# Gate tiles of an expert stage in two buffers, each loaded one four of experts ahead

## Chip, core and metric

The kernel runs on one core of a Trainium2 chip. The metric is the device time of one execution in microseconds; of several executions the median is taken. PE is the matrix engine (PEld its weight loads), DVE the vector engine, ACT the scalar engine, POOL the engine that issues the gathers, and SP the engine whose in-order queue issues all other DMAs.

## The reference, cut to what matters

One decoder layer over 1024 tokens and 16 meta tokens, width 1024: a mixer (latent attention and retention, merged by gates), then an expert layer with 16384 single-neuron experts. The expert layer is what matters here:

```python
x = rmsnorm(h, g_ffn)
# 8 heads choose 16 experts each by product keys: 128 indices eidx and 128 gates per token
act = gelu(einsum('td,tkd->tk', x, peer_u[eidx]))
y = einsum('tk,tkd->td', gates * act, peer_v[eidx])
out = h + y
```

## The kernel before, in words

The tokens are eight blocks of 128. Blocks 0 to 2 take the expert layer by **gathers**: for each of a block's 256 rows of `peer_u` and `peer_v`, POOL issues an indirect DMA of one row per token (tile `row`, four buffers, L1065) and DVE uses it (L1082, L1087). The gathers are background work: `pace` (called by `split_piece`, L221) puts a few of them behind every piece of weights that the main line splits.

Blocks 3 to 7 (640 tokens) take it **densely**, in `dense` (L1128). For each of 128 steps `e`, `scores(e)` (L1150) multiplies 128 experts' rows of `peer_u` with the 640 tokens on PE (line L246 to L248 with output tile `tr`) and writes gelu of it to a tile `gl` (three buffers, L1159). For the first 48 steps this is done early and stored in DRAM as `gl_d`, while `gate_matrix` (L1094) builds the gates of all experts for all 640 tokens in DRAM (`gate_d`). After that the **V stage** begins (`vp` pool, about 2057 us on). It takes 16 groups of eight steps in the order `es`, which mixes fours of steps whose `gl` is loaded from `gl_d` (12 fours) with fours whose scores are computed in this stage (20 fours). Per step:

- `activations(e)` (L1198) computes the scores or loads `gl`.
- `weights(e, gl)` (L1205): at the first step of a four it loads `gt`, the gates of four steps (1280 KB, 10 KB of each partition, DMA line L1209), then DVE multiplies `gl` by them (L1210). ACT rounds the product to `c_hi` and DVE takes the remainder `c_lo` (`split`, L218 and L219; eight buffers each).

When the eight steps of a group are prepared, PE multiplies `c_hi` and `c_lo` with pieces of `peer_v` (raw, three buffers; split to `whi` and `wlo`, three buffers) for the two halves of the width, in accumulators `zacc`, and DVE adds these to `y` (L1243). Each engine works through its own instructions in a fixed order, which the build takes from the program's order and a planner; SP's queue is in order too.

The gate tile has one buffer (`GTB = 1`, L46):

```python
            if e % 4 == 0:
                gt[0] = vp.tile([P, nt, 4, TS], F32, name="gt", bufs=GTB)
                nc.sync.dma_start(gt[0], gate_d[:, :, TS * e:TS * e + 4 * TS].rearrange("n p (e t) -> p n e t", e=4))
            V.tensor_tensor(gl.rearrange("p (n t) -> p n t", t=TS), gt[0][:, :, e % 4],
                            gl.rearrange("p (n t) -> p n t", t=TS), OP.mult)
```

Pools are stacks: `const`, `work`, `wp`, then on the left those of the mixer, and after them `up` (tiles `gl`), the pool of the gate matrix and `vp`. `work` stays open to the end; it holds `zt` (two buffers of 2 KB a partition; L251, L840), used by the mixer alone, and the four retention states (two buffers of 512 B each, L641), used by the mixer alone.

Of the kernel before, what the change touches and what calls it, by code (L numbers as in the profile page):

```python
# [12 lines left out]
F32 = mybir.dt.float32  # L13
BF16 = mybir.dt.bfloat16
# [9 lines left out]
P = 128  # L24
# [9 lines left out]
TW = 512  # L34
# [4 lines left out]
TS = 32  # L39
# [3 lines left out]
RING = 3  # L43
ROWS = 4
SPLIT = 3
GTB = 1  # L46
DELAY = 8.0
STEPS = (((86, 72), (116, 64), (116, 144)), ((112, 90), (112, 90), (112,)), (80, 50))
HEAD = 20
# [94 lines left out]
def hybrid_layer(ctx: ExitStack, tc: tile.TileContext, out, a, dbg=None):  # L144
    nc = tc.nc
    V, S, T, G = nc.vector, nc.scalar, nc.tensor, nc.gpsimd
# [3 lines left out]
    work = ctx.enter_context(tc.tile_pool(name="work", bufs=2))  # L150
    wp = ctx.enter_context(tc.tile_pool(name="wp", bufs=2))
    ps = ctx.enter_context(tc.tile_pool(name="ps", bufs=2, space=PSUM))
    dram = ctx.enter_context(tc.tile_pool(name="dram", bufs=1, space=DRAM))

    gat = ctx.enter_context(tc.tile_pool(name="gat", bufs=1, side="right"))


# [43 lines left out]
    gate_d = dram.tile([DT // TS, P, P * TS], F32, name="gate_d")  # L201
# [46 lines left out]
        T.matmul(o, st[1], mv[0], start=False, stop=last)  # L248

    def square_sum(src, acc):  # L250
        junk = work.tile([P, TW], F32, name="zt").bitcast(BF16)  # L251
        S.activation(junk[:, :src.shape[-1]], src, AF.Square, accum_out=acc)

    def norm_scale(tiles, name):
# [24 lines left out]
    def zacc(name="zacc"):  # L279
        return ps.tile([P, 2, 512], F32, name=name, tag="zacc", bufs=3)  # L280

    def tr():
        return ps.tile([P, TW], F32, name="tr", bufs=2)
# [20 lines left out]
    state = {}  # L304
# [11 lines left out]
    def group(g):  # L316
        blocks = GROUPS[g]
        nbk = len(blocks)
        W = P * nbk
# [270 lines left out]
        def retention(hp):  # L590
# [45 lines left out]
            def add_state(i):  # L636
                pst = tr()
                for s in range(2):
                    T.matmul(pst[64 * s:64 * s + 64, 0:P], qn[:, i, 128 + 64 * s:128 + 64 * s + 64],
                             vr[:, i, P * s:P * s + P], start=True, stop=True)  # L640
                new = work.tile([P, P], F32, name=f"state{hp}")  # L641
                if hp in state:
                    V.tensor_tensor(new, pst[:, 0:P], state[hp], OP.add)
                else:
                    V.tensor_copy(new, pst[:, 0:P])
                state[hp] = new
# [28 lines left out]
            th = rp.tile([P, nbk, 256], F32, name="at")  # L675
# [150 lines left out]
        def merge():  # L826
            mg = own.mg
            for c in range(KD):
                for s, src in enumerate((own.oTs, own.yTs)):
                    pz = zacc()  # L830
                    for j, w in enumerate(split_pieces(a["w_z"][2 * c + s], KD, P)):
                        mm3(pz[:, 0, :W], w, [t[:, j, :W] for t in own.hn], j == 0, j == KD - 1)
                        if j % 2:
                            yield
                    n = len(src)
                    for j, w in enumerate(split_pieces(a["w_ret" if s else "w_mla"][c], n, P)):
                        mm3(pz[:, 1, :W], w, src[j], j == 0, j == n - 1)
                        if j % 2:
                            yield
                    th = work.tile([P, TW], F32, name="zt")[:, :W]  # L840
                    S.activation(th, pz[:, 0, :W], AF.Tanh, scale=0.5)
                    V.scalar_tensor_tensor(th if s else mg[:, c], th, 1.0, pz[:, 1, :W], op0=OP.add, op1=OP.mult)
                    if s:
                        V.tensor_tensor(mg[:, c], mg[:, c], th, OP.add)
# [283 lines left out]
    def dense(xT):  # L1128
        nt = DT // TS
# [4 lines left out]
        for g, blocks in enumerate(GROUPS[NGROUP:-1]):  # L1134
            w = P * len(blocks)
            t = [xdp.tile([P, KD, w], F32R, name=f"x_{n}{g}") for n in ("hi", "lo")]
            per = 1024 // w
            for dst, src in zip(t, xT_d[g]):
                for j in range(0, KD, per):
                    n = min(per, KD - j)  # L1140
# [50 lines left out]
        vp = vps.enter_context(tc.tile_pool(name="vp", bufs=1, reuse_waits="tile"))  # L1191
        ys = []
        for b in range(NGATH, NBLK):
            ys.append(vp.tile([P, D], F32, name=f"y{b}"))
            nc.sync.dma_start(ys[-1], h2_d[b])
        gt = {}

        def activations(e):  # L1198
            if e >= AHEAD:
# [5 lines left out]
        def weights(e, gl):  # L1205

            if e % 4 == 0:
                gt[0] = vp.tile([P, nt, 4, TS], F32, name="gt", bufs=GTB)
                nc.sync.dma_start(gt[0], gate_d[:, :, TS * e:TS * e + 4 * TS].rearrange("n p (e t) -> p n e t", e=4))  # L1209
            V.tensor_tensor(gl.rearrange("p (n t) -> p n t", t=TS), gt[0][:, :, e % 4],  # L1210
                            gl.rearrange("p (n t) -> p n t", t=TS), OP.mult)
            hi = vp.tile([P, DT], F32R, name="c_hi", bufs=CB)
            lo = vp.tile([P, DT], F32R, name="c_lo", bufs=CB)
            split(hi, lo, gl)
            return hi, lo


        es = [4 * n + k for n in sorted(range(P // 4), key=lambda n: (n + 0.5) / AHEAD if 4 * n < AHEAD else
                                        (n + 0.5 - AHEAD / 4) / (P - AHEAD)) for k in range(4)]
        for e0 in range(0, P, GE):  # L1220
            group = es[e0:e0 + GE]
            ne = len(group)
# [65 lines left out]
    for n, now in enumerate(groups):  # L1288
        if n:
            now.open_mix()  # L1290
        now.mix()
        following = groups[n + 1] if n + 1 < len(groups) else None
        now.open_merge(following)
        interleave([now.merge()] + ([following.latents()] if following else []), STEPS[1][n])
        rest = now.output()
    dense(rest)
    finish(1)

# [17 lines left out]
```

## Time and profile before

| | us |
|---|---|
| median of 3 runs | 3613.85 (3611.62 to 3617.17) |
| profiled execution, its own time | 3618.72 |
| its span, first to last instruction | 3616.9 |
| PE busy | 3343.7 (92%) |
| DVE busy | 2788.3 (77%) |
| ACT busy | 1191.6 (33%) |
| POOL busy | 1088.5 (30%) |
| mean granted PE clock, share of full speed | 0.969 |

The span and the rows are those of the profiled execution; its time is 1.8 us longer than its span and 4.9 us longer than the median. Busy time of PE counts overlapping, pipelined instructions once.

### The profile page before, as it was taken

What the parts mean: (1) busy time and instruction counts of PE and PEld (TensorE: products, weight loads), DVE (VectorE), ACT (ScalarE), POOL (GpSimd) and SP (SyncE); (2) the same over time, 40 slices, a digit from 0 to 9 for tenths busy, and PEclk for the clock granted to TensorE, in tenths of its full rate; (3) what the DMA queues carried; (4) which work ended last, traced back from release to release, by engine and by line L of the source; (5) the groups of instructions that cost most, each with busy time, mean ns of one, the idle gap of its engine ahead of it and who ended that gap; (6) DMA issues with size and microseconds to landing.
All of it is one profiled execution on the core that took longest, in us unless ns stands there. A gap on an engine that the chain in (4) does not pass through costs nothing.

```text
span 3616.9 us, 54537 instructions
## 1 busy us (share of the span) xinstructions
PE 3343.7 (92%) x20376; PEld 3023.5 (84%) x20376; DVE 2788.3 (77%) x6698; ACT 1191.6 (33%) x2017; POOL 1088.5 (30%) x772
## 2 busy tenths in 40 slices
PE   8999989998799998999898899999999989999999
PEld 7888988788677898998888687888788878887788
DVE  5645569997896666899999887787778777877776
ACT  3445334544355533233333222222222222222221
POOL 0000000112011121113333355454545544544454
PEclk9999999999899998999999999999999999999999
DMA  3322454467644376455666788898889888988886
GB/s 128 119 81 98 136 189 136 150 211 242 209 145 154 123 261 242 160 174 218 267 252 259 273 313 315 286 321 293 303 281 315 279 288 297 323 298 287 287 298 247
DMA packets 329257, 837.18 MB, mean 231 GB/s; under 512 B 45712, under 2 KB 140688, under 8 KB 326176
## 3 DMA queue, kind: packets, MB, share of 16 engines
q1 hardware_dynamic: 218400, 431.00, 35.4%
q0 software_dynamic: 110592, 402.70, 31.5%
q8 instruction: 160, 2.62, 0.3%
q14 instruction: 105, 0.86, 0.1%
HBM read 755.16 MB, written 78.43 MB: 230 GB/s over the span
## 4 chain that ended last, share of the span: by engine, by line
PE 42%; DVE 20%; issue 16%; DMA 11%; POOL 8%; ACT 3%; POOLq 0%; SPq 0%; DVEq 0%; ACTq 0%
PE zacc L246 9%; PE zacc L248 9%; PE zacc L247 9%; POOL row L1065 8%; DMA row<-in_peer_v_dram,eidx 7%; DVE ob L1120 4%; DVE oa L1119 3%; DVE wlo L219 3%; DVE acc L1087 3%; PE tr L246 3%; PE tr L247 2%; PE tr L248 2%; PE tr L765 2%; DMA gt<-gate_d 2%; PE sc L729 1%
## 5 line engine op out<-in xcount | busy, mean ns | idle before, releaser
L1065 POOL DMA_INDIRECT row<-in_peer_u_dram,eidx x384 | 494.6, 1288 | 1726.3 <-DVE row L1082 837.0
L218 ACT ACTIVATE whi<-raw 128x1024 fp32r<-128x1024 f32 (+2 forms) x508 | 520.7, 1026 | 1263.4 <-PE zacc L248 626.9
L219 DVE TENSOR_TENSOR wlo<-raw,whi 128x1024 fp32r<-128x1024 f32 (+2 forms) x508 | 599.3, 1180 | 328.4 <-ACT whi L218 327.3
L1065 POOL DMA_INDIRECT row<-in_peer_v_dram,eidx x384 | 593.7, 1546 | 772.9 <-DVE acc L1087 643.9
L246 PE MATMUL zacc<-whi,c_hi 128*128 128x512 f32 x1280 | 511.2, 399 | 75.3 <-ACT c_hi L218 59.2
L1087 DVE SCALAR_TENSOR_TENSOR acc<-row,dots,acc 128x1024 f32<-128x1024 f32 x384 | 481.7, 1279 | 92.9 <-DMA row<-in_peer_v_dram,eidx 92.2
L248 PE MATMUL zacc<-whi,c_lo 128*128 128x512 f32 x1280 | 509.1, 398 | 2.0 <-DVE c_lo L219 2.0
L247 PE MATMUL zacc<-wlo,c_hi 128*128 128x512 f32 x1280 | 507.9, 397 | 0.0
L1082 DVE SCALAR_TENSOR_TENSOR row<-row,xn 128x1024 f32<-128x1024 f32 x384 | 463.7, 1219 | 55.3 <-DMA row<-in_peer_u_dram,eidx 54.5
L246 PE MATMUL tr<-xT_hi,whi 128*128 128x384 f32 (+1 forms) x1216 | 417.0, 343 | 17.9 <-ACT gl L1159 16.8
L248 PE MATMUL tr<-xT_hi,wlo 128*128 128x384 f32 (+1 forms) x1216 | 413.9, 340 | 0.0
L247 PE MATMUL tr<-xT_lo,whi 128*128 128x384 f32 (+1 forms) x1216 | 411.8, 339 | 0.0
L246 PEld LDWEIGHTS zacc<-whi,c_hi 128*128 128x128 f32 x1280 | 246.9, 193 | 132.9 <-ACT c_hi L218 62.5
L248 PE MATMUL tr<-x_hi,wlo 128*128 128x256 f32 x1024 | 300.4, 293 | 37.3 <-DVE wlo L219 37.3
L246 PE MATMUL tr<-x_hi,whi 128*128 128x256 f32 x1024 | 299.5, 292 | 11.1 <-ACT whi L218 9.1
L247 PE MATMUL tr<-x_lo,whi 128*128 128x256 f32 x1024 | 297.0, 290 | 0.0
L248 PEld LDWEIGHTS zacc<-whi,c_lo 128*128 128x128 f32 x1280 | 245.7, 192 | 60.0 <-DVE c_lo L219 8.3
L247 PEld LDWEIGHTS zacc<-wlo,c_hi 128*128 128x128 f32 x1280 | 246.7, 193 | 51.3
L246 PE MATMUL zacc<-whi,hn_hi 128*128 128x256 f32 x832 | 251.5, 302 | 3.8 <-DVE vr L679 1.3
L246 PEld LDWEIGHTS tr<-xT_hi,whi 128*128 128x128 f32 x1216 | 232.4, 191 | 20.4 <-ACT gl L1159 18.0
L247 PE MATMUL zacc<-wlo,hn_hi 128*128 128x256 f32 x832 | 239.7, 288 | 1.4 <-DVE wlo L219 1.4
L248 PE MATMUL zacc<-whi,hn_lo 128*128 128x256 f32 x832 | 238.6, 287 | 0.0
(284 smaller groups left out, 6935.6 us busy)
## 6 DMA issues: line engine op xcount, KB each, us to landing
raw<-in_peer_ut_dram SPq DMA_DIRECT2D x128, 512.0 KB, 4.8
raw<-in_peer_vt_dram SPq DMA_DIRECT2D x128, 512.0 KB, 6.6
gate_d<-stage SPq DMA_DIRECT2D x20, 2048.0 KB, 7.4
gt<-gate_d SPq DMA_DIRECT2D x32, 1280.0 KB, 14.6
raw<-in_w_nat_dram SPq DMA_DIRECT2D x72, 512.0 KB, 3.5
raw<-in_w_z_dram SPq DMA_DIRECT2D x48, 512.0 KB, 3.3
gl_d<-gl SPq DMA_DIRECT2D x48, 320.0 KB, 2.2
gl<-gl_d SPq DMA_DIRECT2D x48, 320.0 KB, 6.3
```

Source lines behind the costliest of these rows:

```text
L218: S.activation(hi, src, AF.Copy)
L219: V.tensor_tensor(lo, src, hi.bitcast(F32), OP.subtract)
L246: T.matmul(o, st[0], mv[0], start=first, stop=False)
L247: T.matmul(o, st[0], mv[1], start=False, stop=False)
L248: T.matmul(o, st[1], mv[0], start=False, stop=last)
L729: T.matmul(sc[:, c, 0:w], qh, kT[0:96, k0:k0 + w], start=True, stop=c < nch - 1)
L765: T.matmul(oo, vh[:, c + k], pT[:, k], start=False, stop=c + k == b)
L1065: G.indirect_dma_start(out=row, out_offset=None, in_=table, in_offset=bass.IndirectOffsetOnAxis(ap=eidx[:, k:k + 1], axis=0))
L1082: op = V.scalar_tensor_tensor(row, row, 1.0, xn, op0=OP.mult, op1=OP.mult, accum_out=dots[:, k:k + 1])
L1087: op = V.scalar_tensor_tensor(acc[k % 2], row, dots[:, k:k + 1], acc[k % 2], op0=OP.mult, op1=OP.add)
L1119: V.tensor_scalar(oa[:, t], iota, kt[:, 0, k:k + 1], None, op0=OP.is_equal)
L1120: V.tensor_scalar(ob[:, t], iota, kt[:, 1, k:k + 1], gT[:, k:k + 1], op0=OP.is_equal, op1=OP.mult)
```

## The change

A new pool `mw` holds `zt` and the retention states and is closed when the mixer ends, so that `up`, the gate matrix and `vp` begin 8 KB lower. The gate tile gets two buffers, and the load for a four is issued at the first step of the four before it; the first four's load is issued ahead of the loop over the groups.

```diff
-GTB = 1
+GTB = 2
...
+    mixers = ExitStack()
+    mw = mixers.enter_context(tc.tile_pool(name="mw", bufs=2))
...
     def square_sum(src, acc):
-        junk = work.tile([P, TW], F32, name="zt").bitcast(BF16)
+        junk = mw.tile([P, TW], F32, name="zt").bitcast(BF16)
...
-                new = work.tile([P, P], F32, name=f"state{hp}")
+                new = mw.tile([P, P], F32, name=f"state{hp}")
...
-                    th = work.tile([P, TW], F32, name="zt")[:, :W]
+                    th = mw.tile([P, TW], F32, name="zt")[:, :W]
...
-        gt = {}
+        gts = deque()
+
+        def gate_tile(e):
+            gts.append(vp.tile([P, nt, 4, TS], F32, name="gt", bufs=GTB))
+            nc.sync.dma_start(gts[-1], gate_d[:, :, TS * e:TS * e + 4 * TS].rearrange("n p (e t) -> p n e t", e=4))
...
             if e % 4 == 0:
-                gt[0] = vp.tile([P, nt, 4, TS], F32, name="gt", bufs=GTB)
-                nc.sync.dma_start(gt[0], gate_d[:, :, TS * e:TS * e + 4 * TS].rearrange("n p (e t) -> p n e t", e=4))
-            V.tensor_tensor(gl.rearrange("p (n t) -> p n t", t=TS), gt[0][:, :, e % 4],
+                if e != es[0]:
+                    gts.popleft()
+                if e != es[-4]:
+                    gate_tile(es[es.index(e) + 4])
+            V.tensor_tensor(gl.rearrange("p (n t) -> p n t", t=TS), gts[0][:, :, e % 4],
                             gl.rearrange("p (n t) -> p n t", t=TS), OP.mult)
...
+        gate_tile(es[0])
         for e0 in range(0, P, GE):
...
         rest = now.output()
+    mixers.close()
     dense(rest)
```

## Rows read from the trace of the kernel before

**Rows 1.** The page, chain that ended last: shares by engine, then by line.
```profile
PE 42%; DVE 20%; issue 16%; DMA 11%; POOL 8%; ACT 3%; POOLq 0%; SPq 0%; DVEq 0%; ACTq 0%
PE zacc L246 9%; PE zacc L248 9%; PE zacc L247 9%; POOL row L1065 8%; DMA row<-in_peer_v_dram,eidx 7%; DVE ob L1120 4%; DVE oa L1119 3%; DVE wlo L219 3%; DVE acc L1087 3%; PE tr L246 3%; PE tr L247 2%; PE tr L248 2%; PE tr L765 2%; DMA gt<-gate_d 2%; PE sc L729 1%
```

**Rows 2.** Windows: the stretch before the V stage, and the V stage.
```profile
core 0: us, PE busy (x) PEld busy (x) DVE busy (x) ACT busy (x) POOL busy (x), PEclk, DMA share, GB/s
...
1500.00:2057.00 557.00, 511.62 (x3537) 489.62 (x3536) 537.58 (x1888) 177.15 (x236) 163.56 (x91) 0.98 0.62 230
2057.00:3617.00 1560.00, 1458.22 (x7563) 1287.46 (x7561) 1195.68 (x1439) 360.86 (x489) 781.61 (x553) 0.97 0.86 297
```

**Rows 3.** PE's waits, 2057 to 2090, then 2090 on: us, times, longest.
```profile
PE zacc L246 <- ACT c_hi L218: 14.1, 1, 14.1
...
PE zacc L246 <- ACT c_hi L218: 45.1, 7, 7.6
PE tr L246 <- ACT gl L1159: 18.4, 7, 5.1
PE zacc L246 <- DVE y L1243: 16.1, 10, 3.6
PE zacc L248 <- DVE c_lo L219: 2.0, 8, 0.5
```

**Rows 4.** DVE's waits in the V stage.
```profile
DVE wlo L219 <- ACT whi L218: 108.1, 87, 3.3
DVE gl L1210 <- DMA gt<-gate_d: 95.9, 17, 8.7
DVE acc L1087 <- DMA row<-in_peer_v_dram,eidx: 82.7, 58, 6.0
DVE row L1082 <- DMA row<-in_peer_u_dram,eidx: 54.5, 46, 4.0
```

**Rows 5.** The gate tile's view: its loads, their time to landing.
```profile
L1209 SPq DMA_DIRECT2D gt<-gate_d x32: 370/371/463, 2057.6 to 3518.5; - x32
...
DMA to landing us min/median/max: 8.1/14.6/23.2
```

**Rows 6.** Timeline, one stall: SP, DVE, ACT, PE (start, length, idle before).
```profile
2172.65 0.37 SPq L1209 DMA_DIRECT2D gt<-gate_d  x1
...
2188.06 2.30 DVE L1210 TENSOR_TENSOR gl<-gt,gl 128x640 f32<-128x640 f32 x3 [7.62 <-DMA gt<-gate_d]
...
2188.92 2.21 ACT L218 ACTIVATE c_hi<-gl 128x640 fp32r<-128x640 f32 x3 [11.73 <-DVE gl L1210]
...
2189.71 0.79 PE L246 MATMUL zacc<-whi,c_hi 128*128 128x512 f32 x1 [6.82 <-ACT c_hi L218]
```

**Rows 7.** Windows: three long stretches in which PE hardly waits.
```profile
2290.00:2480.00 190.00, 189.22 (x984) 167.06 (x982) 148.61 (x221) 45.22 (x60) 99.25 (x73) 1.00 0.91 311
2720.00:2870.00 150.00, 150.00 (x795) 133.73 (x794) 121.61 (x117) 36.44 (x49) 84.63 (x59) 0.99 0.90 311
3115.00:3263.00 148.00, 148.00 (x790) 132.15 (x789) 117.03 (x166) 36.64 (x50) 76.06 (x58) 1.00 0.89 312
```

**Rows 8.** SP's own waits in the V stage: the gate loads.
```profile
SPq L1209 <- DVE gl L1210: 56.9, 31, 6.1
```

**Rows 9.** SP's timeline: the two gate loads nearest to each other.
```profile
2087.26 0.37 SPq L1209 DMA_DIRECT2D gt<-gate_d  x1
...
2105.97 0.38 SPq L1209 DMA_DIRECT2D gt<-gate_d  x1
```

**Rows 10.** Windows: first and last of 11 stretches behind stalls; their sum.
```profile
2189.60:2199.00 9.40, 9.07 (x26) 6.82 (x27) 9.40 (x15) 3.22 (x5) 3.28 (x3) 0.65 0.59 191
...
3458.50:3468.00 9.50, 9.24 (x52) 9.24 (x53) 9.50 (x11) 2.82 (x6) 7.54 (x4) 0.82 0.66 221
sum 100.90, PE 96.67 PEld 81.50 DVE 98.47 ACT 34.07 POOL 52.40; mean PE 8.79 PEld 7.41 DVE 8.95 ACT 3.10 POOL 4.76
```

**Rows 11.** Timeline, SP and DVE: a gather waited for beside a gate load.
```profile
2692.01 0.37 SPq L1209 DMA_DIRECT2D gt<-gate_d  x1
...
2703.94 1.28 DVE L1087 SCALAR_TENSOR_TENSOR acc<-row,dots,acc 128x1024 f32<-128x1024 f32 x1 [5.30 <-DMA row<-in_peer_v_dram,eidx]
```

## The prediction, made before the changed kernel was run

> **What bounds the kernel now.** I read the page's chain first [rows 1]. It runs mostly through matmuls and names, as its one large DMA beside the gathers, the load of the gate tile: 2% of the span, some 70 us. That tile exists only in the V stage, so I cut the trace by stage [rows 2]. The V stage is 1560 us; PE is busy in 1458 of them at a mean granted clock of 0.97, DVE in 1196, and the DMA engines are at 0.86. So PE sets the pace there, with about 100 us of holes. PE's waits say what the holes are [rows 3]: 14.1 us once at the start and 45.1 in seven later waits for `c_hi`, 18.4 for a gelu, 16.1 for DVE's additions to `y`, 2.0 for `c_lo`; 95.7 in all. DVE's waits [rows 4] hold the cause: 95.9 us in 17 waits, up to 8.7 each, in which the multiplication by the gates stands waiting for `gt`. Its loads take 14.6 us in the median from issue to landing [rows 5].
>
> One stall shows the link [rows 6]. SP issues the load at 2172.65, when the last multiplication of the four before has freed the one buffer. DVE idles 7.62 us and multiplies at 2188.06, ACT makes `c_hi` at 2188.92, PE restarts at 2189.71 after 6.82 us idle. Where a four's scores are still being computed, the same wait shows as the gelu: three `gl` tiles fill up, ACT can't write the next one, PE has no accumulator. Between the stalls there are long stretches without holes [rows 7]: for 190, 150 and 148 us PE is busy in practically all of the time, at 0.99 to 1.00 of the clock, with DVE at 78 to 81% and the DMA engines at 0.89 to 0.91. Several gate loads fall into these stretches too. They are my picture of the stage after the change.
>
> **The change, part by part.** *Pools.* The tiles of `mw` have the names, sizes and buffer counts they had in `work`, so the mixer issues the same instructions. What is new is that `gl` tiles lie where `zt` and the states lay. Their last readers (the squares of the final norm, the retention) come before the transposed tokens that the first scores read, so nothing new is waited for: 0 us. If that cover failed, it would cost one ACT instruction's wait at the stage's start, under 5 us.
>
> *The loads.* There are still 32 loads of 1280 KB, the same bytes in all. Each of the 31 later ones waits for the last multiplication of the four before, as now, since that frees the second buffer. So in SP's queue each stands where its predecessor's successor stood: SP's 56.9 us of waits there stay as they are [rows 8], and what queues behind (weights, `gl`) is held up neither more nor less. Only the content is one four further on. The two loads nearest to each other are 18.7 us apart [rows 9], more than the 14.6 of a median load, so a tile that is issued a four ahead has landed when it is wanted.
>
> *The stalls.* I take away the seven `c_hi` waits and the gelu waits, 45.1 + 18.4 = 63.5 us. What is late next: DVE was ready 7.62 us before its multiplication, `c_hi` follows 1.6 us after a multiplication starts, so it would have been ready about 0.8 us before PE came (7.62 against 6.82 [rows 6]). That margin is thin; a gather of the usual lateness may reopen a microsecond here and there. I take 0 and keep 15 us (some 11 stalls by 1 to 1.5) as the bad end.
>
> *The clock.* PE restarts slowly. In the 9.4 us behind the stall shown, the granted clock is 0.65, a mix of the two levels of 1.2 and 2.4 GHz [rows 10]. Over 11 such stretches, 100.9 us in all, length times (1 - clock) adds up to 25.8 us; the first gives 9.4 x 0.35 = 3.3, the last 9.5 x 0.18 = 1.7. Without the stalls PE has no such restarts: 25.8 us more.
>
> *The `y` waits.* 16.1 us in ten waits, where DVE comes late to empty the accumulators. Part of the delay is the backlog a gate wait leaves, part is late gathers, which stay. Between 0 and 16.1 I take half, 8.
>
> *The start.* The first gate load can't come sooner: it needs the whole of `gate_d`, whose last part is written just before. The 14.1 us stay. The second load now follows it at once; 1.31 MB at the 311 GB/s of the busy stretches [rows 7] is 4.2 us. Bounds: 0 (behind the first in the queue) and 4.2 (shared evenly); I take 2 lost.
>
> *Gathers beside gate loads.* While DVE stood still it asked for few rows; now gathers run beside all loads. The nearest row is a gather that DVE waited 5.30 us for, 12 us into a gate load [rows 11]. DVE has about 20% of its time free in the stretches of rows 7, in which PE lost nothing, so I take 0 on the path; the other bound is the slow rival below.
>
> The Trainium skill ("DMA: Bandwidth & Descriptors", Queues, rings and completion order) says that each DMA engine takes the queues that have work in turn, a packet at a time. By that rule a gather is slowed by a gate load but never stands behind the whole of it, the term is 0 and the sum below unchanged; by the row alone it could be up to 5.30 us for a load.
>
> Sum: 63.5 + 25.8 + 8 - 2 = 95 us less. The profiled execution is 3618.72 us, so 3523.4 after; it stands 4.87 us above the median of 3613.85, so the median should come to 3518.5, 2.6% faster. The V stage would be 1465 us.
>
> **The rivals.** *The DMA engines bind.* The stage's transfers keep the engines busy for 0.86 x 1560 = 1342 us [rows 2]. My 1465 us need a share of 0.916, a little over the 0.91 of the best long stretch [rows 7]. If no more than the 0.89 of the third is kept up, the stage is 1342 / 0.89 = 1508 us, the gain 52, the time 3562. For it: gathers and gate loads then show as DVE waits. Against: at 0.91 PE still wanted for nothing.
>
> *More goes than I count.* All `y` waits and other half-speed stretches too: 1560 x 0.03 = 47 us of clock loss by the stage's mean [rows 2], 21 over my 25.8, and 8 of `y`: 3490.
>
> *The load isn't ahead in effect.* If SP reached the load only when the next four wants it, DVE would wait as before and the time stay at 3614. For it: SP's queue is in order. Against: spacing [rows 9] and unchanged waits [rows 8].
>
> *Slower.* The gate loads take the gathers' bandwidth while DVE no longer stands still, and `c_lo`, `wlo` and `y` wait behind late rows on DVE's queue. Priced by the row, 5.30 us [rows 11] at each of 31 loads, 164 us, less the 95 gained: 69 slower, 3683. This decides only once DVE's free 20% (9 us of the 46 of a four) no longer covers 5.30 us a four. Rows 7 speak against it.
>
> The skill's rule of turns would shrink this price, which is one more reason for a small chance; no run here shows the turns themselves.
>
> **How the numbers follow.** Forecast 0.62; DMA bound 0.20; more than counted 0.08; no effect 0.06; slower 0.04. A measurement of this kernel tells changes over about 0.2% (7 us) from none. Faster: 0.62 + 0.20 + 0.08 = 0.90; within 0.2%: 0.06; slower: 0.04. The range: downward to 3484, the rival of 3490 and part of the 14.1 us at the start; upward to 3564, which takes in the 15 us of reopened stalls, the `y` waits staying, and the DMA-bound case. A tenth for no effect or slower, and a little of each tail, lies outside.
>
> **What would show it.** Right: DVE's wait for `gt` falls from 95.9 us to the first load's; PE's `c_hi` wait shrinks to one of about 14 us at the stage's start; gelu waits fall below 4; the stage's granted clock rises to 0.99; DMA share 0.91 to 0.92; SP's wait at the gate loads stays near 57. Wrong: DVE's row waits (82.7 + 54.5 us [rows 4]) growing to over 250, or PE waiting for `y`, `c_lo` or `wlo` by tens of microseconds: then the DMA engines or DVE have taken over. If the part before 2057 us changes in length, the pool step is wrong.

## The result, and the profile after

| | before | changed |
|---|---|---|
| median of four runs each, us | 3612.98 (3611.62 to 3617.17) | 3590.64 (3584.88 to 3594.28) |
| profiled execution: its time, its span | 3618.72, 3616.9 | 3594.28, 3592.5 |

The ratio is 0.9935, with a 95% interval of 0.9918 to 0.9952. The change makes the kernel 22 us faster, where 95 were forecast; the time lies above the range. In the changed kernel the lines of the V stage have moved: the gate load is L1202, the load of `gl` L1208, the gate multiplication L1218, the load of raw `peer_v` L1242, the addition to `y` L1252, and the matmuls of the product L248 to L250.

The page's chain first, shares by engine and then by line, as in [rows 1]:

```profile
PE 48%; DVE 20%; issue 15%; DMA 7%; POOL 7%; ACT 3%; POOLq 0%; SPq 0%; DVEq 0%; ACTq 0%
PE zacc L248 10%; PE zacc L249 10%; PE zacc L250 10%; POOL row L1067 7%; DMA row<-in_peer_v_dram,eidx 4%; DVE ob L1122 4%; PE tr L248 3%; PE tr L249 3%; PE tr L250 3%; DVE oa L1121 3%; DVE wlo L221 3%; DVE acc L1089 3%; PE tr L767 2%; PE sc L731 1%; ACT whi L220 1%
```

The gate tile is gone from the chain; so far the change did what it says. The windows, columns as in [rows 2]:

```profile
1500.00:2050.00 550.00, 511.12 (x3544) 491.39 (x3543) 532.18 (x1866) 177.58 (x237) 163.83 (x91) 0.98 0.64 234
2050.00:3592.00 1542.00, 1450.92 (x7569) 1284.80 (x7567) 1194.66 (x1439) 358.68 (x489) 741.15 (x553) 0.97 0.87 301
```

Neither the clock nor the DMA share moved as forecast (0.99 and 0.91 to 0.92): they stand at 0.97 and 0.87. What PE, DVE and SP wait for from 2040 us on (us in total, times, longest) answers to [rows 3, 4, 8]:

```profile
PE zacc L248 <- DVE y L1252: 62.9, 12, 9.4
PE zacc L248 <- ACT c_hi L220: 16.6, 4, 12.4
PE zacc L250 <- DVE c_lo L221: 5.1, 6, 2.4
...
PE tr L248 <- ACT gl L1161: 1.0, 1, 1.0
...
DVE acc L1089 <- DMA row<-in_peer_v_dram,eidx: 72.0, 39, 7.3
DVE gl L1218 <- DMA gl<-gl_d: 70.4, 32, 5.9
DVE row L1084 <- DMA row<-in_peer_u_dram,eidx: 46.7, 36, 5.0
...
DVE gl L1218 <- DMA gt<-gate_d: 2.5, 1, 2.5
...
SPq L1202 <- DVE gl L1218: 102.6, 30, 10.3
```

Read against [rows 3], `c_hi` and gelu have gone almost entirely (of the 16.6 us of `c_hi`, 12.4 are the stage's start), but `y` has risen from 16.1 to 62.9 us. On DVE the wait for the gate tile fell from 95.9 to 2.5, and in its place stands a wait of the same instruction for the other operand, the stored `gl`: 70.4 us where the kernel before had 2.8:

```profile
DVE gl L1210 <- DMA gl<-gl_d: 2.8, 3, 1.8
```

The gathers' waits did not grow (118.7 against 137.2), and SP's wait at the gate loads nearly doubled.

For the sums I cut each trace at the first product of the V stage and its last. "Waits" is PE's idle time in between by the records, "clock" is the length times one minus the mean granted clock.

| kernel | median | first product at | stage | waits | clock | rest |
|---|---|---|---|---|---|---|
| before | 3612.98 | 2082.5 | 1528.2 | 81.6 | 44.9 | 1401.7 |
| changed | 3590.64 | 2075.4 | 1510.9 | 73.2 | 37.5 | 1400.2 |
| e1, pools alone | 3607.13 | 2077.0 | 1527.9 | 84.5 | 47.7 | 1395.7 |
| e5, stored first | 3564.63 | 2097.8 | 1457.8 | 36.4 | 17.1 | 1404.3 |
| e9, chained | 3560.30 | 2070.7 | 1478.4 | 50.2 | 29.0 | 1399.2 |
| e12, chained, stored first | 3533.27 | 2096.6 | 1428.3 | 15.9 | 6.8 | 1405.6 |
| e16, the same but the first group | 3521.66 | 2072.9 | 1442.5 | 24.3 | 14.0 | 1404.2 |
| e15, chained, no gathers | 3465.38 | 2050.8 | 1404.8 | 0 | 0 | 1404.8 |

One of e16's four runs took 4199.47 us, at a granted clock of 0.73 where the others have 0.98, and is left out of its median. The rest is 1396 to 1406 us in every kernel of the table: that is PE's own work in the stage, and all else is PE's waits and the slow clock that goes with them. Of the 24.4 us by which the span fell, 7.1 came ahead of the first product and 17.3 in the stage.

**Where the waits came from.** The 16 groups are of three kinds: computed four then stored four (eight groups), two computed fours (four groups), stored then computed (four groups). All twelve `y` waits of the changed kernel lie in groups of the first two kinds, behind PE's first half: 45.5 us in the first, 17.5 in the second. In one of the first kind, PE's first product runs from 2845.18 us on. The changed kernel's timeline there, DVE, SP and PE in turn (start, length, idle before and its releaser):

```profile
2848.99 0.83 DVE L1218 TENSOR_TENSOR gl<-gt,gl 128x640 f32<-128x640 f32 x1 [3.42 <-DMA gl<-gl_d]
2852.29 1.56 DVE L1218 TENSOR_TENSOR gl<-gt,gl 128x640 f32<-128x640 f32 x2 [2.47 <-DMA gl<-gl_d]
...
2862.15 0.82 DVE L1218 TENSOR_TENSOR gl<-gt,gl 128x640 f32<-128x640 f32 x1 [1.44 <-DMA gl<-gl_d]
...
2877.64 1.28 DVE L1089 SCALAR_TENSOR_TENSOR acc<-row,dots,acc 128x1024 f32<-128x1024 f32 x1 [4.37 <-DMA row<-in_peer_v_dram,eidx]
...
2882.30 1.22 DVE L1252 TENSOR_TENSOR y<-zacc,y 128x512 f32<-128x512 f32 x2
...
2853.87 0.37 SPq L1202 DMA_DIRECT2D gt<-gate_d  x1
...
2883.67 0.77 PE L248 MATMUL zacc<-whi,c_hi 128*128 128x512 f32 x1 [9.03 <-DVE y L1252]
```

SP's gate load tells which multiplication is which: it waits for the computed four's last one, and it is issued at 2853.87, right behind the second multiplication of the pair that began at 2852.29 (2 x 0.82 us, with a start 0.7 us later). So that last multiplication ran some 7.8 us into PE's half, behind two of the stored four's, for each of which DVE stood still until a `gl` landed. In the kernel before, in the same group, it ran first, 2.3 us into the half, which began at 2856.91, and the stored ones behind it:

```profile
2859.18 0.82 DVE L1210 TENSOR_TENSOR gl<-gt,gl 128x640 f32<-128x640 f32 x1
...
2875.88 2.30 DVE L1210 TENSOR_TENSOR gl<-gt,gl 128x640 f32<-128x640 f32 x3 [8.41 <-DMA gt<-gate_d]
...
2894.99 1.28 DVE L1243 TENSOR_TENSOR y<-zacc,y 128x512 f32<-128x512 f32 x2
...
2860.02 0.37 SPq L1209 DMA_DIRECT2D gt<-gate_d  x1
```

There DVE came to `y` 38.1 us into the half, but the half itself took 37.1 with its stall, and PE idled 2.35 us at `y`. The other groups show it too: in the seven computed-stored groups behind the first, this gate load goes out 4.0 to 9.2 us into the half, and 3.1 to 3.6 us into it in the kernel before. With the gate tile there ahead of time, the fixed order that the build gives DVE has changed. The gate load, the later `gl` loads and all of DVE's further work shift with it, DVE reaches `y` 37 us into the half, and PE, whose half now takes 29 us, idles 9.03 us.

### The profile page after: what moved, and what is told of

Its sections match the earlier page's. It is cut to its first block, busy times and chain, and to the rows that moved or that the text cites. A ratio compares the mean times of both kernels' runs of the same rounds, so it can differ in the third digit from the quotient of the medians.

```text
span 3592.5 us, 54520 instructions
## 1 busy us (share of the span) xinstructions
PE 3333.7 (93%) x20376; PEld 3020.7 (84%) x20376; DVE 2785.9 (78%) x6698; ACT 1189.0 (33%) x2017; POOL 1047.2 (29%) x772
## 3 DMA queue, kind: packets, MB, share of 16 engines
q0 software_dynamic: 110592, 402.70, 31.9%
## 4 chain that ended last, share of the span: by engine, by line
PE 48%; DVE 20%; issue 15%; DMA 7%; POOL 7%; ACT 3%; POOLq 0%; SPq 0%; DVEq 0%; ACTq 0%
PE zacc L248 10%; PE zacc L249 10%; PE zacc L250 10%; POOL row L1067 7%; DMA row<-in_peer_v_dram,eidx 4%; DVE ob L1122 4%; PE tr L248 3%; PE tr L249 3%; PE tr L250 3%; DVE oa L1121 3%; DVE wlo L221 3%; DVE acc L1089 3%; PE tr L767 2%; PE sc L731 1%; ACT whi L220 1%
## 5 line engine op out<-in xcount | busy, mean ns | idle before, releaser
L1067 POOL DMA_INDIRECT row<-in_peer_u_dram,eidx x384 | 483.8, 1260 | 1738.8 <-DVE row L1084 834.3
L1067 POOL DMA_INDIRECT row<-in_peer_v_dram,eidx x384 | 563.2, 1467 | 777.1 <-DVE acc L1089 646.6
L248 PE MATMUL zacc<-whi,c_hi 128*128 128x512 f32 x1280 | 511.5, 400 | 79.5 <-DVE y L1252 62.9
L250 PE MATMUL zacc<-whi,c_lo 128*128 128x512 f32 x1280 | 508.9, 398 | 5.1 <-DVE c_lo L221 5.1
L248 PE MATMUL tr<-xT_hi,whi 128*128 128x384 f32 (+1 forms) x1216 | 413.7, 340 | 2.4 <-ACT gl L1161 1.3
L250 PE MATMUL tr<-xT_hi,wlo 128*128 128x384 f32 (+1 forms) x1216 | 410.9, 338 | 0.0
L248 PEld LDWEIGHTS zacc<-whi,c_hi 128*128 128x128 f32 x1280 | 247.0, 193 | 137.1 <-issue 65.3
L250 PE MATMUL tr<-x_hi,wlo 128*128 128x256 f32 x1024 | 301.0, 294 | 30.8 <-DVE wlo L221 30.8
L248 PE MATMUL tr<-x_hi,whi 128*128 128x256 f32 x1024 | 299.2, 292 | 9.0 <-ACT whi L220 9.0
L250 PEld LDWEIGHTS zacc<-whi,c_lo 128*128 128x128 f32 x1280 | 246.3, 192 | 60.4 <-DVE c_lo L221 8.2
L248 PE MATMUL zacc<-whi,hn_hi 128*128 128x256 f32 x832 | 250.9, 302 | 3.8 <-DVE vr L681 1.3
L250 PE MATMUL zacc<-whi,hn_lo 128*128 128x256 f32 x832 | 238.1, 286 | 0.0
L248 PEld LDWEIGHTS tr<-xT_hi,whi 128*128 128x128 f32 x1216 | 230.9, 190 | 4.2 <-DVE xT_lo L279 1.9
```

The lines of the kernel that those rows point to most:

```text
L248: T.matmul(o, st[0], mv[0], start=first, stop=False)
L1067: G.indirect_dma_start(out=row, out_offset=None, in_=table, in_offset=bass.IndirectOffsetOnAxis(ap=eidx[:, k:k + 1], axis=0))
```

## The experiments

Ratios are to the kernel before, run beside each, with 95% intervals; its medians there lay between 3611.44 and 3617.93 us, so that differences of medians and of ratios are not quite the same.

**e1: the pools alone.** The changed kernel with one gate buffer and the load where it was.

```diff
-GTB = 2
+GTB = 1
...
```

> Only the pool move: zt and the retention states in a pool that ends with the mixer; the gate tile keeps its one buffer and is loaded at its own four. The changed kernel reached the V stage 6.9 us earlier than before (its last write of gate_d at 2032.1 us against 2039.1). Theory A: that is the pool move's doing (the tiles of the gate matrix lie 8 KB lower and can be built earlier), so this run is 5 to 9 us faster than before, with DVE's wait for gt still at 90 to 100 us. Theory B: the 6.9 us come from another order of the V stage's planning, and this run is within 3 us of before.

Measured: 3607.13 us, 0.9978 [0.9965, 0.999], some 8 us faster. The stage is as before (1527.9 us), but its first product comes 5.5 us earlier. One tile's view of the gate matrix's vector work shows most of it (its operation, duration, first and last start); the kernel before, then e1:

```profile
L1119 DVE TENSOR_SCALAR oa<-iota,kt x640: 266/275/501, 1633.7 to 2036.9; 128x128 f32<-128x128 f32 x160
```

```profile
L1121 DVE TENSOR_SCALAR oa<-iota,kt x640: 267/274/501, 1415.3 to 2032.8; 128x128 f32<-128x128 f32 x160
```

With its tiles over other memory, the first of this work runs 218 us earlier and the last 4.1. Only the first 16 of the 640 operations run that early; the 17th starts at 1641.5 instead of 1644.5 us, and from there on the lead is 3 to 4 us. The last part of `gate_d` is written at 2035.0 instead of 2039.1 us. Which wait the other memory took away is not shown.

**e2: the gate load at the last step of a four.**

```diff
-                if e != es[-4]:
-                    gate_tile(es[es.index(e) + 4])
+            if e % 4 == 3 and e != es[-1]:
+                gate_tile(es[es.index(e) + 1])
```

> The changed kernel, with the next four's gate load issued at the last step of a four instead of its first, so that the four's own gl loads stand ahead of it in SP's queue. In the changed kernel DVE waits 70.4 us for gl loads in the V stage and PE 62.9 us for y. Theory of the loads: the gl loads that stand behind or beside the gate load became the last to come, hold DVE, and so delay y; then DVE's wait for gl falls under 35 us, PE's wait for y under 35 us, and the time falls by 20 to 45 us against the changed kernel (to about 3550 to 3570). Theory of the gathers: rows are what DVE is late for; then gl waits fall but row waits grow by as much, y waits stay over 50 us and the time moves by less than 10 us. Theory of DVE's own work: nothing changes beyond 5 us.

Measured: 3586.81 us, 0.9912 [0.9889, 0.9934]; `y` waits 63.7, waits for `gl` 71.0. In the built order SP's queue differs from the changed kernel's in a single place, so this run tested next to nothing. The traces answer its question in part: in the changed kernel the 22 loads of `gl` that were issued while a gate load was under way took 7.4 us to landing in the median, the other 26 took 7.1. So a gate load ahead of them is at most a small part of what makes them slow there.

**e3: a fourth buffer for `gl`** (room made by moving four masks to `mw`).

```diff
-            gl = up.tile([P, DT], F32, name="gl", bufs=3)
+            gl = up.tile([P, DT], F32, name="gl", bufs=4)
...
```

> The changed kernel, with four buffers for gl instead of three (room made by moving the masks, used in the mixer alone, into the mixer's pool), so that one more gl load of a four is issued before the gate load. Theory of the loads: DVE's wait for gl falls from 70.4 us to under 45, y waits from 62.9 to under 45, 10 to 30 us faster than the changed kernel. Theory of the gathers or of DVE's own work: within 8 us of the changed kernel, y waits over 50 us.

Measured: 3598.91 us, 0.9953 [0.9939, 0.9968]. DVE's waits for `gl` fell only to 59.1 and PE's for `y` rose to 68.2. More room alone brings no gain; why is not shown, and e11 finds the same with the order put right.

**e4: no gathers.** 756 of the 768 gathers are left out; DVE's work is kept, on the first four rows of each block.

```diff
+            if len(still) < ROWS:
...
-            rows.append(row)
+            rows.append(still[0])
...
```

> The changed kernel without the gathers' transfers: each block fetches its first four rows and DVE then works on these four again and again (the dot takes xn twice, so that values stay finite), so DVE's instructions stay and 756 of 768 gathers are left out. Theory of the gathers: y waits fall from 62.9 us to under 15 and the V stage is 50 us or more shorter. Theory of the loads: gl loads come a little faster with the DMA engines free, but DVE still waits for them 30 us or more, and y waits stay at 20 to 45 us. Theory of DVE's own work: y waits stay at 40 us or more although DVE waits for neither rows nor gl.

Measured: 3467.87 us, 0.959 [0.957, 0.9609]; `y` waits 2.5. The window of its V stage:

```profile
2050.00:3464.00 1414.00, 1406.13 (x7485) 1254.53 (x7483) 1173.07 (x1424) 355.27 (x483) 10.61 (x8) 1.00 0.38 121
```

DVE is as busy as before (1173 us), and PE wants for nothing at a DMA share of 0.38. So it is not the amount of DVE's work by itself that makes `y` late.

**e5 and e8: in each group the stored four first**, in the changed kernel and in the kernel before.

```diff
+        es = [e for e0 in range(0, P, GE) for e in sorted(es[e0:e0 + GE], key=lambda e: e >= AHEAD)]
```

> The changed kernel, with the two fours of each group in the order stored, computed wherever a group mixes them (eight groups are computed, stored in the changed kernel; the four that are stored, computed already show no y wait). Theory of the half's budget: in the first half of a group that ends in a stored four DVE has 23 to 25 us of work (gathers, splits, and the stored four's multiplications and remainders) before y is due about 24 us after the half's first matmul, so any wait for gl or rows makes y late; with the stored four first its DVE work lies beside 60 us of scores, so PE's wait for y falls from 62.9 us to under 30 and the time to 3545 to 3570. Theory of slow transfers alone (the DMA engines are full, so gl and rows come late wherever they are): y waits stay over 45 us and the time stays within 12 us of the changed kernel's 3591.

> The kernel before (one gate buffer, no pool of the mixer) with the same order stored, computed within a group. Both theories have the gate load then fall beside the scores of the previous or the same group, so part of its 45.1 us of c_hi waits goes without a second buffer; I expect 3570 to 3605, and the gate waits of DVE (95.9 us) still over 50. If it comes within 8 us of the changed kernel with the stored four first, the second gate buffer is worth little once the order is right.

Measured: 3564.63 us, 0.9867 [0.985, 0.9885], for the changed kernel, and 3584.36, 0.9917 [0.9901, 0.9933], for the one before, although the first product comes 20 to 22 us later in both. In e5 `y` waits fall to 34.8, where under 30 was expected; of these the computed-stored groups, now stored-computed, have 16.6 (45.5 in the changed kernel) and the computed-computed groups 15.6 (17.5). In this order the second gate buffer and the pools together are worth 18 us by the ratios and 20 by the medians.

**e6: gathers paced otherwise** in the V stage.

```diff
...
+                pacing["rates"] = (0.0, (0.3, 0.65)[s])
```

> The changed kernel, with the same gathers spread otherwise over the V stage: 0.3 instead of 0.5 of the pace in the first halves, 0.65 in the second halves, 0.54 beside the scores, about the same number in all. Theory of the half's budget: some four to five fewer gathers (5 to 6 us of DVE) in each first half, y waits fall from 62.9 us to under 35, 15 to 40 us faster than the changed kernel. Theory of slow transfers alone: the waits only move; y waits over 45 us in all or new waits of PE elsewhere, within 10 us of the changed kernel.

Measured: 3594.02 us, 0.995 [0.9935, 0.9964]. The waits only changed places: `y` 30.3, gelu 37.0, and 96.7 for `gl` on DVE.

**e7: DVE's gather work on half the columns.**

```diff
-                op = V.scalar_tensor_tensor(row, row, 1.0, xn, op0=OP.mult, op1=OP.mult, accum_out=dots[:, k:k + 1])
+                op = V.scalar_tensor_tensor(row[:, :D // 2], row[:, :D // 2], 1.0, xn[:, :D // 2], op0=OP.mult, op1=OP.mult, accum_out=dots[:, k:k + 1])
...
```

The second operation, the addition to `acc`, is cut in half in the same way.

> The changed kernel, with DVE's two operations of the gathers done on half of the columns (the other half is left out); every transfer stays. Theory of the half's budget: DVE's work in the first halves falls by some 5 us (nine operations at half of 1.25 us), so with the same transfers and the same or longer waits for gl and rows PE's wait for y falls under 25 us and the V stage from 1511 us to 1440 or less. Theory of slow transfers alone: DVE just waits longer; y waits over 45 us, V stage over 1485 us.

Measured: 3523.15 us, 0.9751 [0.973, 0.9773], but some 45 us of that lie ahead of the stage (first product at 2030.7). The stage itself is 1487.0 us, and `y` waits are still 47.6, with 90.1 us of DVE waiting for `gl`. With much less work DVE stands longer at slow loads (70.4 us for `gl` in the changed kernel). A theory of mine that DVE's budget in a half was the limit fell here in its plain form, which counted the work and not the waits.

**e9: the multiplications kept in the program's order.** This is the test of the theory that came out of the timeline.

```diff
+        def behind(op, *before):
+            for b in before:
+                tc.add_manual_dep(op.ins, b.ins.name, mybir.DependencyInfo(
+                    mybir.DependencyClass.NoSync, mybir.DependencyReason.DATA), reason="order")
...
+            op = V.tensor_tensor(gl.rearrange("p (n t) -> p n t", t=TS), gts[0][:, :, e % 4],
...
+            behind(op, *gated)
+            gated[:] = [op]
```

Here `op` is the gate multiplication, and `behind` fixes its place on DVE after the one before; nothing is waited for that was not.

> The changed kernel with one thing more: each gate multiplication of DVE is kept behind the one before it in the program's order, so that in a computed-stored group the stored four's multiplications can't stand ahead of the computed four's last one. Nothing is waited for that wasn't. Theory 'order': in the changed kernel DVE stands at the stored four's first multiplications for slow loads of gl while the computed four's last one, which frees the gate buffer and a gl buffer, stands behind them. It expects that last multiplication back at 2 to 3 us behind the start of PE's half (7.8 us in the changed kernel), SP's wait at the gate loads down from 102.6 us to 55 to 75, PE's waits for y down from 62.9 us to under 35, and a time of 3555 to 3575 us. Rival 'slow loads alone': the loads of gl are late wherever DVE waits for them; waits for gl stay above 60 us, PE's waits for y above 50, time within 8 us of the changed kernel's 3590.6.

Measured: 3560.3 us (3557.05 to 3565.05), 0.9865 [0.9847, 0.9883]: 30 us faster than the changed kernel by the medians, 25 by the ratios. The same group, where PE's first product starts at 2822.20; DVE, then SP, then PE:

```profile
2824.46 0.82 DVE L1224 TENSOR_TENSOR gl<-gt,gl 128x640 f32<-128x640 f32 x1
2825.99 0.83 DVE L1224 TENSOR_TENSOR gl<-gt,gl 128x640 f32<-128x640 f32 x1 [0.72 <-DMA gl<-gl_d]
2827.74 0.83 DVE L1224 TENSOR_TENSOR gl<-gt,gl 128x640 f32<-128x640 f32 x1 [0.92 <-DMA gl<-gl_d]
...
2837.38 1.65 DVE L1224 TENSOR_TENSOR gl<-gt,gl 128x640 f32<-128x640 f32 x2 [1.88 <-DMA gl<-gl_d]
...
2825.30 0.37 SPq L1208 DMA_DIRECT2D gt<-gate_d  x1
...
2854.34 0.76 PE L248 MATMUL zacc<-whi,c_hi 128*128 128x512 f32 x1 [4.74 <-DVE y L1260]
```

The computed four's last multiplication is back at 2.3 us into the half, the gate load goes out at 3.1 instead of 8.7, and PE's gap at `y` is 4.74 instead of 9.03. Over the stage:

```profile
PE zacc L248 <- DVE y L1260: 48.0, 10, 8.9
...
DVE gl L1224 <- DMA gl<-gl_d: 46.6, 22, 5.7
...
SPq L1208 <- DVE gl L1224: 55.7, 30, 7.9
```

SP's wait at the gate loads is back at 55.7, near the 56.9 of [rows 8], and the time is in the range of the order theory. The rival is out. But `y` still holds 48.0 us where under 35 was expected: order carries 25 to 30 us of the missing 73, and something else the rest. The group shown gained more than any other. Of the `y` waits, the computed-computed groups lost 15.0 us (17.5 to 2.5) and the eight computed-stored groups none (45.5 to 45.4): there DVE comes to `y` 1.9 us sooner, but PE's half is as much shorter, since the 9.4 us that PE waited inside these halves fell to 1.0.

**e10 and e11: two additions to e9.** In e10 the first half's additions to `y` are kept ahead of the next group's multiplications; e11 has four buffers for `gl`.

```diff
...
+                    if not s:
+                        gated.append(op)
```

> The kernel before in this list, and besides the first half's additions to y kept ahead of the next group's gate multiplications on DVE. Theory 'order': the y waits of the computed-computed groups (2 to 7 us each), where the next group's stored multiplications stand ahead of y, go too: 5 to 20 us faster than the chained kernel. Against it: a multiplication held behind y starts its group's c_hi later, so PE's waits for c_hi and gelu rise by as much as those for y fall, and the time stays within 8 us of the chained kernel's.

> The chained kernel with four buffers for gl (in the changed kernel, unchained, the fourth buffer brought no gain: 3598.9). Theory 'order': the fourth buffer lets the loads of gl start a multiplication earlier, but only once the multiplications are in the program's order; waits for gl under 45 us, 5 to 15 us faster than the chained kernel. Rival 'slow loads alone': with four as with three buffers the same, within 5 us.

Measured: 3560.26 us, 0.9859 [0.9843, 0.9876], and 3572.79 us, 0.9897 [0.988, 0.9914]. In e10 `y` waits stay (49.0) and 5.2 us of gelu wait come up, as the second expectation had it. In e11 DVE waits less for `gl` (35.7) but `y` rises to 61.8: a miss for the order theory, which had expected a gain. I did not follow up why.

**e12: e10 with the stored four first.**

> The chained kernel with y ahead, and in each mixed group the stored four first (alone, without the chain, that order gave 3564.6). If the order stored-computed gained because it takes away the computed-stored groups, in which the multiplications changed places, the chain adds little to it: 3550 to 3570. If it gained for another reason (loads of gl issued in a quieter stretch), the two add up: 3530 to 3550.

Measured: 3533.27 us, 0.9792 [0.9775, 0.981]. The two add up, as the second expectation had it, though not for the reason named there, as the `gl` loads are hardly faster (6.8 us in the median against 7.2). PE and DVE in its V stage:

```profile
PE zacc L248 <- DVE y L1261: 2.5, 2, 2.3
...
DVE gl L1224 <- DMA gl<-gl_d: 2.7, 3, 2.0
```

So the waits for `y` and for `gl` are both gone. What the stored-first order adds on top of e10 is where DVE's work stands. In e9 five gate multiplications with their five `c_lo`, 10 x 0.82 = 8.2 us, lie within PE's first half of a computed-stored group; with the stored four first, only one pair does.

**e13 and e14: short loads of `gl`**, in the changed kernel and in e9. Each load of a stored `gl` moves only the last `TS` columns, and the multiplication reads these for all. `TS` is 32, so that is a twentieth of the 640 columns, 16 KB of 320; the 64 KB of the expectation are an error of mine.

```diff
-            nc.sync.dma_start(gl, gl_d[e])
+            nc.sync.dma_start(gl[:, DT - TS:], gl_d[e, :, DT - TS:])
...
+                            gl.rearrange("p (n t) -> p n t", t=TS) if e >= AHEAD else
+                            gl[:, DT - TS:].unsqueeze(1).to_broadcast([P, nt, TS]), OP.mult)
```

> The changed kernel, in which each load of a stored gl moves only the columns of the last block of tokens (64 KB for 320 KB); the gate multiplication reads those columns for all five blocks, so its size stays, and the stored steps' weights of the other four blocks are wrong. The order of the instructions stays as in the changed kernel. Theory: the new late thing is the load of gl (70.4 us of DVE's waits), which holds up everything behind it to y. With short loads DVE's waits for gl fall under 30 us, PE's waits for y from 62.9 to under 30, and the time to 3535 to 3560 us. Rival 'gathers': DVE's waits for rows of the gathers carry y; they rise as those for gl fall, PE's waits for y stay above 50, time within 12 us of 3590.6.

> The same short loads in the chained kernel (3560.3 us, PE's waits for y still 48.0 where under 35 was expected). If what is left of those waits is the loads of gl too (46.6 us of DVE's waits there), y falls under 20 us and the time to 3525 to 3545 us. If it is the gathers, whose transfers stand in the same queues of data, y stays above 38 and the time within 10 us of the chained kernel's.

Measured: 3557.02 us, 0.9838 [0.9815, 0.9861], and 3554.9 us, 0.9823 [0.9795, 0.9852]. PE and DVE in e13, then in e14:

```profile
PE zacc L248 <- DVE y L1253: 44.1, 11, 9.7
...
DVE gl L1218 <- DMA gl<-gl_d: 38.5, 20, 3.9
```

```profile
PE zacc L248 <- DVE y L1261: 45.1, 9, 9.2
...
DVE gl L1224 <- DMA gl<-gl_d: 31.9, 14, 4.7
```

Shorter loads alone give the changed kernel 34 us, about as much as the chain; where the loads are short, the chain brings only 2 us more (e14 against e13; 5 by the ratios). Both remedies cure the same delay, DVE standing at `gl`: in e13 too the `y` waits of the computed-computed groups fall to 3.8 us, and those of the computed-stored groups stay at 40.3. The expected amounts of e13 (waits for `gl` under 30, `y` under 30) were missed, the time was met. And the bytes of `gl` are not the rest: `y` stays at 45.1 in e14. (The gathers, which its expectation puts in the same queues as these loads, have a queue of their own in the profile; what the two share is the 16 DMA engines, with 53% of their time from 2050 to 3600 us for the gathers' queue and 33% for the loads' in the changed kernel.)

**e15: e9 without gathers.** The edits of e4 and e9 together.

> The chained kernel with 756 of the 768 gathers left out (the vector work on their rows is kept; blocks 0 to 2 come out wrong). Without the chain, leaving them out gave 3467.9 us and y waits of 2.5 us. If the chain only puts right what slow loads spoil, it brings nothing here: 3460 to 3475 us. If the order costs by itself, it brings 10 us or more.

Measured: 3465.38 us, 0.9583 [0.9562, 0.9603], against 3467.87 in e4. Where transfers are quick the order costs next to nothing. In e15 PE waits for nothing in the stage, although DVE has the same work there.

**e16: e12, but the first group computed-stored.**

```diff
-        es = [e for e0 in range(0, P, GE) for e in sorted(es[e0:e0 + GE], key=lambda e: e >= AHEAD)]
+        es = [e for e0 in range(0, P, GE) for e in sorted(es[e0:e0 + GE], key=lambda e: e >= AHEAD and e0 > 0)]
```

> The chained kernel with y ahead and the stored four first, as in the run that gave 3533.3 us, but the first group as in the changed kernel, with its computed four first. In that run the first product of the stage came at 2096.6 us, 21 us later than in the changed kernel, since the first group's computed four can't be begun early when it stands second. Theory: that delay is the first group's order alone; the first product comes at 2070 to 2078 us and the time falls to 3508 to 3518. Rival: the delay only moves to the second group, 3525 to 3540 us.

Measured: 3521.66 us, 0.9733 [0.9706, 0.9759], the fastest kernel here that computes everything. The first product comes at 2072.9 us, as expected; the time is 4 us above the range given, since the stage is 14 us longer than e12's:

```profile
PE zacc L248 <- DVE y L1261: 12.8, 6, 4.5
PE tr L248 <- ACT gl L1161: 11.3, 4, 6.4
...
DVE acc L1089 <- DMA row<-in_peer_v_dram,eidx: 110.3, 83, 5.9
...
DVE row L1084 <- DMA row<-in_peer_u_dram,eidx: 60.7, 52, 4.1
...
DVE gl L1224 <- DMA gl<-gl_d: 1.5, 3, 0.7
```

The gathers' waits on DVE are larger than in any kernel above (171.0 against 118.7 in the changed one), and yet PE waits for `y` a fifth as long as there. The loads of `gl` are no faster either (7.5 us in the median against 7.2). DVE now has the time for both. The windows of e16's V stage show the forecast's numbers reached, clock 0.99, DMA share 0.91:

```profile
2050.00:3521.00 1471.00, 1426.96 (x7545) 1269.47 (x7543) 1193.38 (x1437) 359.79 (x488) 760.29 (x551) 0.99 0.91 315
```

One table sums it up: the time from PE's start of a first half to DVE's first addition to `y`, and what fills it, in us, mean over the computed-stored groups but the first (in e16 the same seven groups, stored first). What is left over is short waits for ACT; a wait that began before the half is counted whole.

| | before | changed | e9 | e14 | e15 | e16 |
|---|---|---|---|---|---|---|
| to the first addition to `y` | 35.5 | 33.8 | 31.9 | 31.5 | 24.9 | 26.6 |
| DVE's work in it | 22.6 | 23.5 | 23.2 | 23.1 | 23.0 | 19.0 |
| its waits for the gate tile | 7.7 | 0 | 0 | 0 | 0 | 0 |
| its waits for `gl` | 0 | 6.7 | 4.2 | 3.1 | 0.9 | 0 |
| its waits for rows | 3.4 | 3.8 | 3.5 | 4.2 | 0 | 5.9 |

From PE's start of a first half to its start of the second it is 27.2 us where PE does not wait in between. The change took 1.7 us off DVE's way to `y`, while PE's half shrank from some 37 us to 27 to 32. What DVE is late by, PE now waits for. Some 23 us of work fit into 27.2 us as long as loads come at once (e15), and no longer with some 9 us or more of waits; neither the work alone nor the loads alone make `y` late. e16 has longer waits for rows than the changed kernel and is in time because 4.5 us of work and all waits for `gl` have left the half.

## Why the prediction was wrong

*Pools, 0 us: wrong, by some 8 us of gain.* The cover I named was about waits of the stage's tiles; what moved was the gate matrix's vector work, and with it the stage's first product, by 5.5 us (e1).

*The stalls, 63.5 us: right as a removal.* Within the stage `c_hi` fell from 45.1 to 4.3 and gelu from 18.4 to 1.0, 58.2 us in all.

*The stalls, "what is late next ... I take 0": this is the step that failed.* I looked only at `c_hi`, 0.8 us ahead of PE. Two things stood behind the gate tile. The multiplication has a second operand: `gl`, whose load takes 7.2 us in the median of the changed kernel, was hidden under the gate wait (2.8 us of waits) and came out at 70.4. Slow loads of it were there before: the 12 that were issued while a gate load was under way took 13.8 us in the median, the other 36 took 5.7. And `y`, 35.5 us into a half, was hidden because the half itself was stretched to some 37 by the stall I removed. `y` rose by 46.8 us and `c_lo` by 3.1; my bad end for this was 15.

*An assumption not written down: that DVE's order stays.* It changed, and that alone costs 25 to 30 us (e9). With the order put right, what stays is the stored fours' preparation within PE's half (e12, e16: 39 us more by the medians of e9 and e16, 48 by the ratios). That the build put the stored multiplications forward because the gate tile was there is argued; that their place costs the time is shown.

*The loads, "SP's 56.9 us stay": wrong, 102.6.* The release is the same instruction as before, but that instruction itself now stands behind two waits for `gl`. In e9 it is 55.7. That a tile issued a four ahead has landed when it is wanted held, with 2.5 us of waits left, though I had set a median load against the spacing and not the longest, 23.2 us [rows 5].

*The clock, 25.8 us: 7.4 came.* The sum held only for a stage without stalls. New stalls bring their own restarts: in the table of stages the loss is between 0.43 and 0.58 of the waits in every kernel that waits. With e16's 24.3 us of waits it is 14.0, 30.9 us less than before.

*The y waits, 8 us gained: wrong in sign,* 46.8 lost.

*The start, 2 lost: 1.7 gained,* 12.4 against 14.1 for the first `c_hi`; with the 5.5 of e1 that is 7.2, about the 7.1 us ahead of the first product.

*Gathers beside gate loads, 0: the waits for rows did not grow* (118.7 against 137.2), and the slower rival with its 164 us did not show. Yet without gathers PE hardly waits in the stage (e4, e15): the waits for rows are gone there, and the `gl` loads take 4.6 us (e15) instead of 7.2, so the gathers' traffic slows them.

Sum as measured: 58.2 - 46.8 - 3.1 + 7.4 + 7.1 = 22.8 us; the span fell by 24.4; the stage's rest is 1.5 us shorter, which I leave open. The rival of the bound DMA engines was not it either: the share was 0.87, with holes, and e16 moves the same bytes at 0.91. That e16, at 3521.66, comes near the forecast of 3518.5 us does not bear out the sum: it took three further edits, and one of them, the stored four first, gave the kernel before 27 to 30 us without the change (e8). What the chain and that order together would give with one gate buffer was not run. The sign that I named as "wrong" in advance, PE waiting for `y` by tens of microseconds, is the one that came.

## What to carry to other kernels

When a wait for one operand goes, list every operand of the waiting instruction and every later instruction of its in-order engine, each with its own time of arrival; a wait of 2.8 us beside one of 95.9 is a measure of the cover, not of the transfer. Compare the order of instructions on each engine before and after an edit that only moves a load or a buffer, and keep work that stands behind slow loads out of the stretch in which the bounding engine next needs that engine. For such a stretch add the second engine's work and its waits, and hold the sum against the time that the bounding engine takes without stalls (here 23 and 10 us against 27). Count a removed stall twice (the wait and, in these kernels, about half as much in clock), and a new one twice as well.

## What the runs showed of the hardware that I had not expected

The time of a small load under this traffic is hardly its own bytes. The load of `gl`, issued by SP, took 7.2 us in the median with 320 KB in the changed kernel, 5.7 us with a twentieth of the columns (16 KB) in e13, and 4.6 us with all 320 KB but without gathers in e15:

```profile
gl<-gl_d SPq DMA_DIRECT2D x48, 320.0 KB, 7.2
```

```profile
gl<-gl_d SPq DMA_DIRECT2D x48, 320.0 KB, 4.6
```

The Trainium skill ("DMA: Bandwidth & Descriptors", Anatomy of one DMA — SWDGE (gpsimd) path) gives a fit of 2.0 us plus the bytes over 436 KB per us for the other way of issue; an estimate by it is 2.75 us for 320 KB and 2.04 for 16 KB. The measured difference between the two, 1.5 us, is more than the fit's 0.7, and the level is over twice as high at a DMA share of 0.87; the measurement decides. Part of the time from issue to landing goes with loads that SP issued before: in e15 the 20 loads of `gl` that were issued while a gate load was under way took 6.6 us in the median, the other 28 took 3.8.
